# Scaling x by token ahead of time and splitting u on another engine, in the first stage of a hybrid decoder block

## The chip, the cores and the metric

The kernel runs on one core of a Trainium2 chip. A core has five engines with queues of their own: PE (TensorE, the matrix unit), DVE (VectorE), ACT (ScalarE), POOL (GpSimd) and SP (SyncE, which here only issues DMAs). Each engine works through its queue strictly in order; an instruction that waits holds up all that stands behind it on its engine. The metric is the device time of one execution in microseconds, the median of several runs.

## What is computed

One layer of a decoder block for 512 tokens of width 2048, in fp32. What matters here is its beginning:

```python
mod = jax.nn.silu(c) @ w_ada[l] + b_ada[l]          # (1, 12288): six vectors of 2048
sh1, sc1, g1, sh2, sc2, g2 = jnp.split(mod, 6, axis=-1)
u = _rmsnorm(h, norm_attn[l]) * (1 + sc1) + sh1     # 512 x 2048
z = u @ w_in                                        # then cut into queries, keys, values, gates
... two attentions, y @ w_out, a gated residual, SwiGLU, a last RMSNorm
```

`x` is (1, 512, 2048), `w_ada` (2048, 12288), `w_in` (2048, 5664).

## The kernel before

**Layout.** Activations lie transposed: a tile holds 128 features (partitions) by 512 tokens, so x and u are 16 tiles each (`xT`, `u`). To keep fp32 precision on fast matmuls every operand is split into a high part (rounded to fp32r) and a low part (the rest), and each product is three matmuls: high x high, low x high, high x low. ACT makes the high part and DVE the low part: of a weight chunk `wr` as `wh` (L244) and `wl` (L249), of u as `uh` (L416) and `ul` (L420).

**First stage.** x is loaded and transposed, and the token scale `rstd1` (one factor for each token) is made, in the first 25 us. Then 64 steps stream the two sixths of `w_ada` that give shift and scale, in eight blocks of eight steps. A step loads one tile `ad` of 128 x 2 x 512 (512 KB, in two DMAs). A block gives shift and scale of two feature tiles, and so two tiles of u. Within a block:

- DVE multiplies the rows of the `ad` tiles by SiLU(c) and adds them up in `acc` (L531 for the first, L533 for the others), two instructions for a tile; in some steps (`on_pe`) PE takes the second of the two as a matmul into a PSUM row (L540), which ACT copies out at the end (`row`, L544).
- Then PE sums over partitions (L552): eight small matmuls over `row`, eight over `acc`. The text calls this "the sums of block j".
- DVE adds the bias (`mod`, L560) and makes `a_vec` (L400), and for each of the two feature tiles `mt` = x * a_vec * rstd1 (L414). ACT makes `uh` from `mt` (L416), DVE then `ul` (L420).
- PE multiplies the new u with chunks of `w_in` in units of three matmuls (L278, L279, L280), 144 units in the stage. They go into eight PSUM banks: S0 (tags `pss`, `pso`, first for one half of the query columns, moved out by `keep_half` after block 3, then for the compressed keys and values) and S1 (`psmm`).

**What sets the order.** In this stage the queues stand as the code emits them. `LAGS` says how many steps after a block's last load its sums, its `mod`, its `ul` and its S1 units come; `KEEP` how many units may be left before a step emits two rather than one (three from block 4 on). `w_pairs` loads the chunks of `w_in` for a block (`wr`, at most three of a kind at a time), in the middle of a block. Eight `ad` tiles may be held at a time, so SP runs at most eight tiles ahead of DVE. The tables of sine and cosine (`extra_work`, L431 to L452) are made on DVE in blocks 1 to 3.

After the stage x is written to DRAM (`xsp`, L590), for which SP first has to issue three chunks of `w_in`, the last of which waits for a low part of block 7; the next stage goes on with the same u, and the rest of the kernel (attentions, FFN) isn't touched: from there on the instructions of both kernels stand in the same order on all engines.

Of the kernel before, what the change touches and what calls it, by code (L numbers as in the profile page):

```python
# [9 lines left out]
F32 = mybir.dt.float32  # L10
F32R = mybir.dt.float32r
I32 = mybir.dt.int32
AF = mybir.ActivationFunctionType
OP = mybir.AluOpType
AX = mybir.AxisListType

P = 128
T = 512
NT = T // P
D = 2048  # L20
ND = D // P
# [4 lines left out]
EPS = 1e-6  # L26
ADW = 8
LAG = 2
LAGS = 2, 3, 4, 6
LAGS0 = 1, 2, 3, 0  # L30
KEEP = 12
R_C, R_D, R_F, R_V = 1.0, 1.0, 1.0, 0.6
SCALE = HD ** -0.5
NCMP = 31
# [45 lines left out]
def hymba_block(ctx: ExitStack, tc: tile.TileContext, x, c, positions, w_ada, b_ada, norm_attn,  # L80
                norm_ffn, w_in, b_fgate, cmp_pos, w_kc1, w_kc2, w_vc1, w_vc2, beta_fox, beta_nsa,
                w_out, w_gate, w_up, w_down, final_norm, cst, out):
    nc = tc.nc
# [10 lines left out]
    act = pool(aw, "act")  # L94
# [7 lines left out]
    def uid(s):  # L102
        n_uid[0] += 1
        return f"{s}_{n_uid[0]}"
# [9 lines left out]
    def split_ap(t):  # L114
        return t.bitcast(F32)
# [287 lines left out]
    def act_tile(name, i):  # L403
        h = act.tile([P, T], F32R, tag="ah", name=uid(name + "h"), bufs=ND)
        l = act.tile([P, T], F32R, tag="al", name=uid(name + "l"), bufs=ND)
        return h, l

    def modulate(which, i, src, rb, pl):
        return modulate_b(*modulate_a(which, i, src, rb, pl))

    def modulate_a(which, i, src, rb, pl):
        sh = mod[:, (0 if which == 0 else 3) * ND + i:(0 if which == 0 else 3) * ND + i + 1]
        t = pl.tile([P, T], F32, tag="mt", name=uid("mt"), bufs=2)
        nc.vector.scalar_tensor_tensor(t, src, a_vec[:, which, i:i + 1], rb, op0=OP.mult, op1=OP.mult)  # L414
        h, l = act_tile("u", i)
        nc.scalar.activation(h, t, AF.Identity, bias=sh)  # L416
        return h, l, t, sh

    def modulate_b(h, l, t, sh):
        nc.vector.scalar_tensor_tensor(l, t, sh, split_ap(h), op0=OP.add, op1=OP.subtract)  # L420
        return h, l

    cosT = sinT = None

# [32 lines left out]
    p_cmp = [cols(w_in, C_KC, 512)]  # L457
    p_s1 = [cols(w_in, C_KS, 256), cols(w_in, C_KW, 128)]
    part = None
    u = []  # L460
    NJ = ND // 2
    HJ = NJ // 2

    def w_pairs(j):
        s1 = fetch_w(p_s1, j, src=early, width=3 * P, bufs=2)
        if j < HJ:
            return [fetch_w(p_qn, j), s1]
        i = 2 * (j - HJ)
        return [fetch_w(p_cmp, i), s1, fetch_w(p_cmp, i + 1)]
# [24 lines left out]

    def on_pe(n):
        j, r = divmod(n, 8)
        return r < 7 if j == 0 else 2 <= r < (6 if j <= HJ else 4)

    tiles, accs, rows, sums, halves, fetched, todo = {}, {}, {}, {}, {}, {}, []
    extra_work = tables()  # L500
    AT, AT_END = {0: 0, 1: 1, 3: 2}, {0: 0, 1: 1, 5: 2}
    step = 0
    while step < SLOTS + 8 or todo:
        j, r = divmod(step, 8)
        if j < NJ:
            tiles[step] = early.tile([P, 2, T], F32, tag="adw", name=uid("ad"), bufs=ADW)
            for i, sec in ((0, 1), (1, 0)):
                c0 = sec * D + j * 256
                nc.sync.dma_start(tiles[step][:, :, i * 256:(i + 1) * 256],
                                  w_ada[:, c0:c0 + 256].rearrange("(q p) n -> p q n", p=P)[:, 2 * r:2 * r + 2, :])  # L510
        if r == (2 if j else 7) and j < NJ:
            fetched[j] = w_pairs(j)
        if j == 1 and r < 2:
            fetched[0][r].high()
        i = AT.get(r, 3) if j < NJ else AT_END.get(r, 3)
# [7 lines left out]
        if 0 <= n < SLOTS:  # L523
            jj, q0 = n // 8, 2 * (n % 8)
            if q0 == 0:
                accs[jj] = early.tile([P, T], F32, tag="acc", name=uid("acc"), bufs=2)
            acc = accs[jj]
            for q in range(1 if on_pe(n) else 2):
                sc1 = sl[:, q0 + q:q0 + q + 1]
                if q0 + q == 0:  # L530
                    nc.vector.tensor_scalar(acc, tiles[n][:, q, :], sc1, None, op0=OP.mult)  # L531
                else:
                    nc.vector.scalar_tensor_tensor(acc, tiles[n][:, q, :], sc1, acc, op0=OP.mult, op1=OP.add)  # L533
        n = step - 2
        if 0 <= n < SLOTS and on_pe(n):
            jj, q = n // 8, 2 * (n % 8) + 1
# [10 lines left out]
        if n is not None:  # L547
            jj = n // 8
            sums[jj] = bank("mm")
            for av, one in ((rows.pop(jj), one_col[0:1, :]), (accs.pop(jj), one_col)):  # L550
                for i in range(4):
                    nc.tensor.matmul(sums[jj][:, i:i + 1], av[:, i * P:(i + 1) * P], one,  # L552
                                     start=one is not one_col and i == 0, stop=one is one_col,
                                     skip_group_check=True)
        n = due(step, 1)
        if n is not None:
            jj = n // 8
            for k2, sec in ((0, 1), (1, 0)):
                m0 = sec * ND + 2 * jj
                nc.vector.tensor_tensor(mod[:, m0:m0 + 2], sums[jj][:, 2 * k2:2 * k2 + 2], b_mod[:, m0:m0 + 2],  # L560
                                        op=OP.add)
            scale_vec(0, jj * 2, 2)
            pend = [modulate_a(0, i, xT[:, i, :], rstd1, early) for i in (2 * jj, 2 * jj + 1)]
            if jj == 0:
                halves[0] = [fetched[0][0]()]
        n = due(step, 2)
        if n is not None:
            u.extend([modulate_b(*h) for h in pend])
            jj = n // 8
            if jj == 0:  # L570
                halves[0].append(fetched[0][1]())
            if jj < HJ:
                todo += units(halves[jj][0], jj, S0, ND // 2) + units(halves[jj][1], jj, S1, ND)
            if jj == HJ - 1:
                todo.append(keep_half)
# [851 lines left out]
```

## Time and profile before

| | us |
|---|---|
| median of 3 runs | 2454.54 |
| lowest and highest | 2450.6 to 2454.8 |
| the profiled execution | 2450.92 |
| its span | 2448.0 |
| first stage, last matmul | 191.10 |

The profile belongs to one execution, and all sums below are made in it: its own time is 2.9 us over its span and 3.6 us under the median. To read it: busy times are sums over instructions; a row of the timeline gives start, duration, engine, line, and in brackets how long the engine had been idle and what it had waited for. A matmul's duration includes its way through the array, so the time that one matmul costs in a row of many is read from start to start. PEclk is the granted clock of TensorE as a share of 2.4 GHz; it has two levels, 1.2 and 2.4 GHz.

### The profile page before, as it was taken

The page shows a single profiled execution, that of the slowest core. Times are in us where ns is not written, and L with a number is a line of the kernel's source. Part 1 is how long each engine was busy: PE and PEld are TensorE (multiplying, and loading weights), DVE is VectorE, ACT ScalarE, POOL GpSimd, SP SyncE. Part 2 cuts the span into 40 slices and gives each one's busy share as a digit, 9 for nine tenths or more (in the row PEclk, how much of TensorE's full clock was granted, in tenths as well). Part 3 has the DMA queues.
Part 4 walks back from the last instruction along what each step waited for, and adds up shares of the span by engine and source line. Part 5 has one row for each costly group of instructions (what it writes and reads, how often), then busy time and mean ns, then how long its engine had stood idle before and what let it go on. Part 6 is the DMA issues. An engine that isn't in the chain of part 4 may idle for free.

```text
span 2448.0 us, 38482 instructions
## 1 busy us (share of the span) xinstructions
PE 2355.1 (96%) x14717; PEld 2100.4 (86%) x14717; DVE 1579.6 (65%) x2711; ACT 1016.0 (42%) x1531; POOL 341.5 (14%) x370
## 2 busy tenths in 40 slices
PE   6998999999999989889999999999999999999998
PEld 4677887888888767789999999999999888888887
DVE  6876786887755576596777777777776643333333
ACT  3224544344423332365555555555555422222133
POOL 0003002000001121251222121212221100000010
PEclk8998999999999999999999999999999999999999
DMA  9864743463554277559898989898988644333322
GB/s 332 283 198 147 205 139 95 130 190 117 180 174 129 85 249 253 186 122 237 211 231 215 228 213 232 220 225 212 221 200 193 192 151 141 123 120 121 102 95 101
DMA packets 322713, 440.31 MB, mean 180 GB/s; under 512 B 26224, under 2 KB 217552, under 8 KB 322528
## 3 DMA queue, kind: packets, MB, share of 16 engines
q1 hardware_dynamic: 289104, 348.21, 44.0%
q0 software_dynamic: 31120, 85.45, 18.7%
q10 hardware_dynamic: 2304, 4.20, 0.5%
q8 instruction: 115, 1.88, 0.3%
q14 instruction: 70, 0.57, 0.1%
HBM read 340.18 MB, written 28.38 MB: 151 GB/s over the span
## 4 chain that ended last, share of the span: by engine, by line
PE 54%; DVE 1%; DMA 0%; issue 0%; ACT 0%; SPq 0%; DVEq 0%; ACTq 0%
PE py L1161 12%; PE py L1164 11%; PE py L1163 11%; PE psmm L278 3%; PE psmm L279 3%; PE psmm L280 3%; PE pss L278 2%; PE pss L279 2%; PE pss L280 2%; PE pso L279 1%; PE pso L278 1%; PE pso L280 1%; DMA wr<-in_w_down_dram 0%; PE pso L1058 0%; DVE ul L1141 0%
## 5 line engine op out<-in xcount | busy, mean ns | idle before, releaser
L249 DVE TENSOR_TENSOR wl<-wr,wh 128x1024 fp32r<-128x1024 f32 (+2 forms) x211 | 239.0, 1133 | 381.5 <-ACT wh L244 378.4
L244 ACT CAST wh<-wr 128x1024 fp32r<-128x1024 f32 (+2 forms) x211 | 199.5, 948 | 502.7 <-PE psmm L279 199.7
L1164 PE MATMUL py<-uh,ls 128*128 128x256 f32 x1408 | 397.6, 282 | 3.6 <-DVE ls L1107 3.6
L1163 PE MATMUL py<-ul,hs 128*128 128x256 f32 x1408 | 397.6, 282 | 2.2 <-DVE ul L1141 2.2
L1161 PE MATMUL py<-uh,hs 128*128 128x256 f32 x1408 | 398.4, 283 | 1.0 <-DVE ev L1178 0.5
L1107 DVE TENSOR_TENSOR ls<-sum,hs 128x1024 fp32r<-128x1024 f32 x176 | 215.2, 1223 | 196.5 <-ACT hs L1101 196.5
L1101 ACT CAST hs<-sum 128x1024 fp32r<-128x1024 f32 x176 | 184.5, 1049 | 377.3 <-PE py L1163 257.5
L1163 PE MATMUL py<-ul,hx 128*128 128x256 f32 x1056 | 298.8, 283 | 4.0 <-DVE ul L1141 4.0
L1161 PE MATMUL py<-uh,hx 128*128 128x256 f32 x1056 | 299.3, 283 | 1.7 <-ACT uh L1140 1.4
L1164 PE MATMUL py<-uh,lx 128*128 128x256 f32 x1056 | 298.3, 282 | 0.0
L1164 PEld LDWEIGHTS py<-uh,ls 128*128 128x128 f32 x1408 | 267.0, 190 | 4.7 <-DVE ls L1107 4.6
L1163 PEld LDWEIGHTS py<-ul,hs 128*128 128x128 f32 x1408 | 267.0, 190 | 3.3 <-DVE ul L1141 3.3
L1161 PEld LDWEIGHTS py<-uh,hs 128*128 128x128 f32 x1408 | 267.1, 190 | 2.7 <-DVE ev L1178 1.3
L1097 POOL DMA_DIRECT2D lx<-raw x176 | 156.2, 887 | 580.2 <-ACT lx L1096 419.4
L1163 PEld LDWEIGHTS py<-ul,hx 128*128 128x128 f32 x1056 | 200.8, 190 | 5.1 <-DVE ul L1141 5.1
L1161 PEld LDWEIGHTS py<-uh,hx 128*128 128x128 f32 x1056 | 200.6, 190 | 2.2 <-ACT uh L1140 1.7
L1164 PEld LDWEIGHTS py<-uh,lx 128*128 128x128 f32 x1056 | 200.7, 190 | 0.0
L386 DVE SCALAR_TENSOR_TENSOR acc<-ad,sl,acc 128x512 f32<-128x512 f32 x180 | 141.6, 787 | 43.2 <-DMA ad<-in_w_ada_dram 41.4
L1092 ACT CAST hx<-raw 128x768 fp32r<-128x768 f32 x176 | 144.3, 820 | 11.3 <-DMA raw<-in_w_gate_dram 11.3
L1096 ACT ACTIVATE lx<-raw 128x768 fp32r<-128x768 f32 x176 | 148.1, 841 | 1.8 <-DMA raw<-in_w_gate_dram 1.8
L278 PE MATMUL psmm<-fh,wh 128*128 128x512 f32 x352 | 137.0, 389 | 0.0
L280 PE MATMUL psmm<-fh,wl 128*128 128x512 f32 x352 | 136.9, 389 | 0.0
(441 smaller groups left out, 5284.3 us busy)
## 6 DMA issues: line engine op xcount, KB each, us to landing
lx<-raw POOLq DMA_DIRECT2D x176, 384.0 KB, 5.2
ad<-in_w_ada_dram SPq DMA_DIRECT2D x128, 512.0 KB, 4.1
raw<-in_w_up_dram SPq DMA_DIRECT2D x176, 256.0 KB, 4.2
raw<-in_w_gate_dram SPq DMA_DIRECT2D x176, 256.0 KB, 4.5
wr<-in_w_down_dram SPq DMA_DIRECT2D x88, 512.0 KB, 3.6
ad<-in_w_ada_dram SPq DMA_DIRECT2D x128, 256.0 KB, 6.0
wr<-in_w_in_dram SPq DMA_DIRECT2D x104, 256.0 KB, 3.5
wr<-in_w_in_dram SPq DMA_DIRECT2D x24, 512.0 KB, 4.4
```

The lines of the kernel that those rows point to most:

```text
L244: nc.scalar.copy(wh[:, :, sc], v)
L249: nc.vector.tensor_tensor(held[1][:, :, sc], v, split_ap(held[0])[:, :, sc], op=OP.subtract)
L278: nc.tensor.matmul(dst, wh[:, k, w], ah, start=first, stop=False)
L279: nc.tensor.matmul(dst, wh[:, k, w], al, start=False, stop=False)
L280: nc.tensor.matmul(dst, wl[:, k, w], ah, start=False, stop=last)
L1096: nc.scalar.activation(lx[s], raw[s][:, 1:4, :], AF.Copy, scale=-1.0)
L1097: nc.gpsimd.dma_start(split_ap(lx[s]), raw[s][:, 1:4, :], accum_op=OP.add)
L1101: nc.scalar.copy(hs[s], sums[s])
L1107: nc.vector.tensor_tensor(ls[s], sums[s], split_ap(hs[s]), op=OP.subtract)
L1161: nc.tensor.matmul(o, wh[:, wi, js], vh[:, vi, :], start=k == 0 and j == 0, stop=False, skip_group_check=True)
L1163: nc.tensor.matmul(o, wh[:, wi, js], vl[:, vi, :], start=False, stop=False, skip_group_check=True)
L1164: nc.tensor.matmul(o, wl[:, wi, js], vh[:, vi, :], start=False, stop=k == KG - 1, skip_group_check=True)
```

## The change

- `norm_x` on DVE multiplies each of the 16 tiles of x by `rstd1` ahead of time, into `xn`, in steps 4 to 18 (blocks 0 to 2). `xn` uses the buffers that `ul` will have.
- ACT makes `uh` and `mt` from `xn` with a_vec as scale and the shift as bias, two instructions a tile (L418), and DVE `ul` = mt - uh as a plain subtraction (L423). `ul` comes five steps after the block's last load, not four (`LAGS`), and S1 units seven, not six. `KEEP` falls from 12 to 9.
- High parts of weights (`wh`) are cast by ACT two steps before DVE makes their low parts, so ahead of the copy of `row` and no longer behind it. `w_pairs` comes one step later.
- PE takes rows of `w_ada` in five steps of block 0 (seven before), four of blocks 1 to 4 as before, and none of blocks 5 to 7 (two each before). There `row` is gone, DVE takes both halves, and the sums are eight matmuls instead of sixteen.

```diff
-LAGS = 2, 3, 4, 6
+LAGS = 2, 3, 5, 7
-KEEP = 12
+KEEP = 9
...
-    def modulate_a(which, i, src, rb, pl):
-        sh = mod[:, (0 if which == 0 else 3) * ND + i:(0 if which == 0 else 3) * ND + i + 1]
-        t = pl.tile([P, T], F32, tag="mt", name=uid("mt"), bufs=2)
-        nc.vector.scalar_tensor_tensor(t, src, a_vec[:, which, i:i + 1], rb, op0=OP.mult, op1=OP.mult)
-        h, l = act_tile("u", i)
-        nc.scalar.activation(h, t, AF.Identity, bias=sh)
-        return h, l, t, sh
-
-    def modulate_b(h, l, t, sh):
-        nc.vector.scalar_tensor_tensor(l, t, sh, split_ap(h), op0=OP.add, op1=OP.subtract)
-        return h, l
+    u = []
+    xn = [act.tile([P, T], F32, tag="al", name=f"xn{i}", bufs=ND) for i in range(ND)]
+
+    def norm_x(i):
+        nc.vector.tensor_tensor(xn[i], xT[:, i, :], rstd1, op=OP.mult)
+
+    def modulate(i):
+        h = act.tile([P, T], F32R, tag="ah", name=uid("uh"), bufs=ND)
+        t = early.tile([P, T], F32, tag="mt", name=uid("mt"), bufs=2)
+        for dst in (h, t):
+            nc.scalar.activation(dst, xn[i], AF.Identity, scale=a_vec[:, 0, i:i + 1], bias=mod[:, i:i + 1])
+        return h, t
+
+    def modulate_low(h, t):
+        l = act.tile([P, T], F32R, tag="al", name=uid("ul"), bufs=ND)
+        nc.vector.tensor_tensor(l, t, split_ap(h), op=OP.subtract)
+        u.append((h, l))
...
-        return r < 7 if j == 0 else 2 <= r < (6 if j <= HJ else 4)
+        return r < 5 if j == 0 else j <= HJ and 2 <= r < 6
...
+    norms = {4: (0, 1), 5: (2,), 6: (3,), 8: (4, 5)}
+    norms.update({9 + i: (6 + i,) for i in range(10)})
...
-        if r == (2 if j else 7) and j < NJ:
+        if r == (3 if j else 7) and j < NJ:
             fetched[j] = w_pairs(j)
+        i = {7: 0, 0: 1, 1: 2}.get(r, 3)
+        if i < 3 and 1 <= j - (r < 7) < NJ and i < len(fetched[j - (r < 7)]):
+            fetched[j - (r < 7)][i].high()
...
+        if step in norms:
+            for i in norms[step]:
+                norm_x(i)
...
-            for av, one in ((rows.pop(jj), one_col[0:1, :]), (accs.pop(jj), one_col)):
+            srcs = ([(rows.pop(jj), one_col[0:1, :])] if jj in rows else []) + [(accs.pop(jj), one_col)]
+            for av, one in srcs:
...
-            pend = [modulate_a(0, i, xT[:, i, :], rstd1, early) for i in (2 * jj, 2 * jj + 1)]
+            pend = [modulate(i) for i in (2 * jj, 2 * jj + 1)]
...
-            u.extend([modulate_b(*h) for h in pend])
+            for p in pend:
+                modulate_low(*p)
```

Where the instructions stand now. First DVE, from the last `ad` tiles of block 0 to the first `ul`; `acc_292` and `acc_308` are block 0's sum, `wl_334` and `wl_357` the low part of the first chunk. Before:

```order
L533 SCALAR_TENSOR_TENSOR acc_292<-ad_320,sl,acc_292 128x512 x2
L531 TENSOR_SCALAR acc_356<-ad_330,sl 128x512
L533 SCALAR_TENSOR_TENSOR acc_356<-ad_330,sl,acc_356 128x512
L560 TENSOR_TENSOR mod<-psmm_341,vec 128x2 x2
L400 SCALAR_TENSOR_TENSOR a_vec<-mod,vec 128x2
L414 SCALAR_TENSOR_TENSOR mt_362<-xT,a_vec,rstd_269 128x512
L414 SCALAR_TENSOR_TENSOR mt_367<-xT,a_vec,rstd_269 128x512
L249 TENSOR_TENSOR wl_334<-wr_326,wh_333 128x1024
L533 SCALAR_TENSOR_TENSOR acc_356<-ad_350,sl,acc_356 128x512 x2
L420 SCALAR_TENSOR_TENSOR ul_365<-mt_362,mod,uh_364 128x512
```

and in the changed kernel:

```order
L540 SCALAR_TENSOR_TENSOR acc_308<-ad_343,sl,acc_308 128x512 x2
L412 TENSOR_TENSOR xn_282<-xT,rstd_269 128x512
L412 TENSOR_TENSOR xn_283<-xT,rstd_269 128x512
L538 TENSOR_SCALAR acc_378<-ad_353,sl 128x512
L540 SCALAR_TENSOR_TENSOR acc_378<-ad_353,sl,acc_378 128x512
L412 TENSOR_TENSOR xn_284<-xT,rstd_269 128x512
L571 TENSOR_TENSOR mod<-psmm_363,vec 128x2 x2
L400 SCALAR_TENSOR_TENSOR a_vec<-mod,vec 128x2
L249 TENSOR_TENSOR wl_357<-wr_349,wh_356 128x1024
L540 SCALAR_TENSOR_TENSOR acc_378<-ad_372,sl,acc_378 128x512 x2
L412 TENSOR_TENSOR xn_285<-xT,rstd_269 128x512
L423 TENSOR_TENSOR ul_400<-mt_386,uh_385 128x512
```

Three products of x by the token scale stand ahead of `mod`, one between it and the first `ul`, and the two `mt` behind `mod` are gone from DVE.

On ACT, block 1: the copy of `row`, the casts of the two chunks, and u. Before:

```order
L430 CAST posi<-posi 128x512
L544 COPY row_434<-psmm_403 1x512
L244 CAST wh_444<-wr_379 128x1024
L244 CAST wh_457<-wr_376 128x768
L416 ACTIVATE uh_492<-mt_490,mod 128x512
```

and in the changed kernel:

```order
L433 CAST posi<-posi 128x512
L244 CAST wh_465<-wr_417 128x1024
L554 COPY row_472<-psmm_432 1x512
L244 CAST wh_482<-wr_414 128x768
L418 ACTIVATE uh_523<-xn_280,mod,a_vec 128x512
L418 ACTIVATE mt_524<-xn_280,mod,a_vec 128x512
```

The first cast has moved ahead of the copy that waits for PE, and each tile of u has two instructions.

On PE, around the sums of block 7 (`row_1266`, `acc_1171`; now `acc_1196`). Before:

```order
L280 MATMUL psmm_282<-uh_1214,wl_1168 128x512
L552 MATMUL psmm_1324<-cs,row_1266 128x1 x4
L552 MATMUL psmm_1324<-cs,acc_1171 128x1 x4
L278 MATMUL psmm_283<-uh_1214,wh_1167 128x512
L279 MATMUL psmm_283<-ul_1215,wh_1167 128x512
```

and in the changed kernel:

```order
L280 MATMUL psmm_298<-uh_1225,wl_1175 128x512
L563 MATMUL psmm_1342<-cs,acc_1196 128x1 x4
L278 MATMUL psmm_299<-uh_1225,wh_1174 128x512
L279 MATMUL psmm_299<-ul_1267,wh_1174 128x512
L280 MATMUL psmm_299<-uh_1225,wl_1175 128x512
```

The sums over `row` are gone, and with them the matmuls over `ad` that fed them. Between the sums of successive blocks, from the start of u to the end of the stage, PE has 8, 11, 13, 17, 23, 24, 24 and 24 units before the change and 10, 11, 13, 15, 23, 24, 24 and 24 behind it.

## Rows read from the trace of the kernel before

**Rows 1.** Windows by block: busy us (count) of PE, PEld, DVE, ACT, POOL; clock, DMA, GB/s.

```profile
36.54:60.02 23.48, 17.14 (x55) 11.87 (x56) 18.23 (x29) 4.15 (x6) 0.00 (x0) 0.72 1.08 345
60.02:77.01 16.99, 14.79 (x59) 10.69 (x58) 16.81 (x31) 3.64 (x5) 0.00 (x0) 0.90 0.98 312
77.01:94.58 17.57, 16.23 (x64) 11.91 (x63) 16.40 (x29) 6.07 (x8) 0.00 (x0) 0.89 0.97 315
...
133.92:154.28 20.36, 20.36 (x93) 16.06 (x93) 16.32 (x24) 4.69 (x6) 0.00 (x0) 1.00 0.95 303
...
174.66:191.10 16.44, 16.44 (x72) 13.43 (x72) 5.64 (x9) 3.40 (x5) 0.00 (x0) 1.00 0.67 236
```

**Rows 2.** Waits of PE from 25 to 191 us: total, times, longest.

```profile
PE psmm L552 <- DVE acc L533: 5.5, 3, 2.2
PE psmm L552 <- ACT row L544: 3.1, 1, 3.1
PE pss L279 <- DVE ul L420: 2.4, 1, 2.4
...
PE pss L278 <- DVE part L482: 0.9, 1, 0.9
PE pss L278 <- ACT part L484: 0.8, 1, 0.8
```

**Rows 3.** Timeline of ACT, then DVE, then PE, around the sums of block 1.

```profile
51.70 0.58 ACT L544 COPY row<-psmm 1x512 f32<-1x512 f32 x1 [12.03 <-PE psmm L540]
52.19 1.77 ACT L244 CAST wh<-wr 128x1024 fp32r<-128x1024 f32 x2
...
53.26 1.23 DVE L249 TENSOR_TENSOR wl<-wr,wh 128x1024 fp32r<-128x1024 f32 x1 [4.86 <-ACT wh L244]
...
52.98 1.05 PE L552 MATMUL psmm<-cs,row 1*128 1x1 f32 x8
55.99 1.05 PE L552 MATMUL psmm<-cs,acc 128*128 128x1 f32 x8 [1.96 <-DVE acc L533]
...
57.48 0.63 PE L279 MATMUL psmm<-ul,wh 128*128 128x512 f32 x1
57.90 0.63 PE L280 MATMUL psmm<-uh,wl 128*128 128x512 f32 x1
...
61.33 1.02 PE L540 MATMUL psmm<-ad,sl 128*128 128x512 f32 x2
...
62.42 0.40 PE L279 MATMUL psmm<-ul,wh 128*128 128x512 f32 x1
```

**Rows 4.** Timeline of PE: sums of block 4 and the stage's last matmul.

```profile
109.99 1.05 PE L552 MATMUL psmm<-cs,row 1*128 1x1 f32 x8
110.96 1.05 PE L552 MATMUL psmm<-cs,acc 128*128 128x1 f32 x8
...
190.88 0.39 PE L280 MATMUL pso<-uh,wl 128*128 128x512 f32 x1
```

**Rows 5.** Timeline of DVE in block 0, then PE's first matmul with a low part.

```profile
30.41 1.54 DVE L533 SCALAR_TENSOR_TENSOR acc<-ad,sl,acc 128x512 f32<-128x512 f32 x2 [0.74 <-DMA ad<-in_w_ada_dram]
34.45 0.49 DVE L531 TENSOR_SCALAR acc<-ad,sl 128x512 f32<-128x512 f32 x1 [2.50 <-DMA ad<-in_w_ada_dram]
...
36.54 0.22 DVE L560 TENSOR_TENSOR mod<-psmm,vec 128x2 f32<-128x2 f32 x2 [0.81 <-PE psmm L552]
...
41.71 0.79 PE L279 MATMUL pss<-ul,wh 128*128 128x512 f32 x1 [2.36 <-DVE ul L420]
```

**Rows 6.** Groups of instructions, 25 to 191 us: busy us, mean ns, idle before.

```profile
L533 DVE SCALAR_TENSOR_TENSOR acc<-ad,sl,acc 128x512 f32<-128x512 f32 x89 | 66.7, 750 | 4.9 <-DMA ad<-in_w_ada_dram 2.9
L414 DVE SCALAR_TENSOR_TENSOR mt<-xT,a_vec,rstd 128x512 f32<-128x512 f32 x16 | 11.3, 748 | 0.4
L416 ACT ACTIVATE uh<-mt,mod 128x512 fp32r<-128x512 f32 x16 | 11.1, 724 | 53.3 <-DVE mt L414 53.3
```

**Rows 7.** Groups of instructions in the first 300 us: a subtraction of this shape.

```profile
L622 DVE TENSOR_TENSOR cA<-cr,cA 128x512 fp32r<-128x512 f32 x8 | 5.2, 686 | 0.1
```

More of the change, by code (lines that the diff above doesn't have):

```diff
@@ L406, in act_tile @@
         return h, l
-    def modulate(which, i, src, rb, pl):
-        return modulate_b(*modulate_a(which, i, src, rb, pl))
-    def modulate_a(which, i, src, rb, pl):
-        sh = mod[:, (0 if which == 0 else 3) * ND + i:(0 if which == 0 else 3) * ND + i + 1]
-        t = pl.tile([P, T], F32, tag="mt", name=uid("mt"), bufs=2)
-        nc.vector.scalar_tensor_tensor(t, src, a_vec[:, which, i:i + 1], rb, op0=OP.mult, op1=OP.mult)
-        h, l = act_tile("u", i)
-        nc.scalar.activation(h, t, AF.Identity, bias=sh)
-        return h, l, t, sh
-    def modulate_b(h, l, t, sh):
-        nc.vector.scalar_tensor_tensor(l, t, sh, split_ap(h), op0=OP.add, op1=OP.subtract)
-        return h, l
+    u = []
[12 more added lines that the diff above has]
+        u.append((h, l))
     cosT = sinT = None
@@ L459, in hymba_block @@
     part = None
-    u = []
     NJ = ND // 2
@@ L549, in hymba_block @@
             sums[jj] = bank("mm")
-            for av, one in ((rows.pop(jj), one_col[0:1, :]), (accs.pop(jj), one_col)):
+            srcs = ([(rows.pop(jj), one_col[0:1, :])] if jj in rows else []) + [(accs.pop(jj), one_col)]
+            for av, one in srcs:
                 for i in range(4):
                     nc.tensor.matmul(sums[jj][:, i:i + 1], av[:, i * P:(i + 1) * P], one,
-                                     start=one is not one_col and i == 0, stop=one is one_col,
+                                     start=i == 0 and one is srcs[0][1], stop=one is one_col,
                                      skip_group_check=True)
```

## The prediction

> **What bounds the kernel now.** I read the page first: PE is busy for most of the span, so what a change in the first stage is worth is time that PE gets back there. Then the windows cut at each block's `mod` [rows 1]. From the first `mod` at 36.54 us to about 110 us PE is busy for 73 to 92% of a block and DVE is nearly full in two blocks (16.81 of 16.99 us, 16.40 of 17.57), while the core loads 312 to 345 GB/s. From block 4's sums on it is the other way round: in the window from 133.92 us, one of three alike, PE is busy for all of the 20.36 us at the full clock, and DVE has time left. So there are two halves, paced by DVE and the chain of waits around it, and by PE.
>
> The list of PE's waits [rows 2] says what it lost in the first half: 5.5 us for `acc` in three sums, 3.1 us for `row`, 2.4 us for a first `ul`. The timeline of block 1 shows the chain [rows 3]: ACT stands 12.03 us at the copy of `row`, which waits for PE's last rows of `w_ada`; the casts queued behind it start at 52.19 us, DVE sits idle for 4.86 us until the first is done, the last `acc` stands behind that, and PE waits 1.96 us for it. Then matmuls start 0.42 us apart (57.48, 57.90) and later 0.24: the clock had fallen to 1.2 GHz. By the granted clock in rows 1 (0.72, 0.90, 0.89) some 20 us of these three blocks ran at the lower level.
>
> **Prices.** 72 matmuls took 16.44 us in the last window [rows 1]: 0.228 us each, 0.69 a unit. A `w_ada` row on PE: from 61.33 to 62.42 us stand two records of L540, one matmul of the program, and one of a unit [rows 3], so 1.09 - 0.23 = 0.86 us. Eight small sums: 109.99 to 110.96 us, 0.97 us [rows 4]. On DVE an `acc` step, `mt` and `ul` take 0.75 us and a subtraction of the same size 0.69 [rows 6, 7]; since their ends overlap, one costs 0.66 to 0.73 us and 0.61 from start to start.
>
> **From the sums of block 4 on.** Before, this takes 109.99 to 191.10 us [rows 4, 1], 81.1 us, with 95 units. The change takes off six rows of `w_ada`, 6 x 0.86 = 5.2 us, and three times eight sums over `row`, 2.9 us. Of the waits for `part` (0.9 and 0.8 us [rows 2]) about 1.4 us go: six units (4.1 us) now stand between the last unit that fills S0 and the first that needs it empty, and the two copies on ACT, behind a cast (1.0 us) and four activations (2.8 us), come 0.3 us too late. Left: 81.1 - 5.2 - 2.9 - 1.4 = 71.6 us. This needs DVE to keep up: its 16.32 us of block 6 [rows 1] lose two `mt` (1.4) and gain two `acc` steps (1.5), 16.4 to 16.8 us, against 24 units and 0.97 us on PE, 17.5 us. DMA must bring 5.6 MB a block (eight tiles, two chunks, one of 384 KB), 320 GB/s; rows 1 show 303 to 345 where nobody waited for it, and at 303 the block takes 18.6 us, 1.1 too long, which for three blocks comes out of the some 10 us by which tiles land ahead of their use. The added waits: a cast waits for its buffer until 14 units after the sums, then `wl` and the last `acc` follow (1.0 + 1.2 + 1.5 us), 3.5 us before PE needs them. Behind that cast on ACT stands only work of the next block.
>
> **From the first u to the sums of block 4.** Step by step, before in brackets.
> - Block 0. The idle 0.74 us of DVE before each tile [rows 5] takes the first products by `rstd1`; tile 7, here from 30.41 us, ends at 32.7 (31.95). Three products (1.8 us) and tile 8, which lands at 34.45 us, stand before `mod`: 36.3 us (36.54). `mt` is gone there, but a low part of a chunk, the next tile and one product stand before `ul`: it ends at 40.65 us, and PE's second matmul, which waits for it, goes then (41.71 [rows 5]).
> - Block 1. PE has ten units, not eight: the 11.3 us from 41.71 to 52.98 us [rows 5, 3] for eight units and four rows, partly at the low clock, and 1.4: 40.65 + 12.7 = 53.3 us. DVE's nine further products, 9 x 0.61 = 5.5 us, fill the hole of 4.86 us [rows 3], which is gone since the cast no longer stands behind `row`. Its last `acc` ends at 52.6 us, so PE doesn't wait for it. `mod` follows at 58.6 (60.02).
> - Block 2. PE has four units and a row after the sums (55.2 us), then needs a new u. `ul` follows `mod` by 3.6 us (three instructions of tables, two of `acc`, itself): 62.2 us. **PE stands 3.1 us** from 58.9, and I add 2.0 us for a clock at the lower level, as after the wait in rows 3. DVE needs 16.99 us less two `mt` and the shorter `ul`, 15.5: `mod` at 74.1 (77.01).
> - Blocks 3 and 4. DVE: 17.57 - 0.96 idle - 1.46 = 15.15, `mod` at 89.3 (94.58). PE has seven and eight units and three rows each before it needs a new u (7.4 and 8.1 us, against `ul` 4.3 and 4.6 us after the sums), so it doesn't stand. From 62.2 us: 35 units (24.2), 11 rows (9.5), two sums (3.9), clock 2.0, in all 39.6: **block 4's sums at 101.8 us (109.99)**. Without the lower clock 99.8; with a wait and a lower clock as in rows 3 (1.96 + 1.9) in both blocks 109.5.
>
> **Sum.** Stage end at 101.8 + 71.6 = 173.4 us against 191.1: 17.7 us. The next stage's first waits hang on `xsp`, which follows block 7's last `wl`; that comes 5.2 us after the sums' end rather than 4.9, since ACT now makes four activations (0.7 us each) before the last `ul`. That takes 0.4: 17.3 us. The profiled execution would take 2450.9 - 17.3 = 2433.6 us; the median lies 3.6 above it, so **2437 us**. ACT's sixteen further activations, 16 x 0.72 = 11.6 us, lie beside other work: ACT is busy for 4 to 6 us a block [rows 1].
>
> One price has no row: an activation with both scale and bias from memory. Bounds from rows are 0.72 us [rows 6], with the bias alone from memory, and 0.86, if the second operand adds what the first has over the plain copy of 0.58 us [rows 3]; less is excluded, since the work is the same. I take 0.72. The upper end moves `xsp` by four times 0.14, 0.6 us, and nothing else, since at the one stall DVE's own instructions end later than ACT's. The Trainium skill ("ScalarE: Activation LUTs", section "What ACT_TABLE_LOAD costs") says that each operand read per partition adds about 93 ns; by it four activations would take 0.4 us longer, an estimate from that page, and the sum would be 16.9 us instead of 17.3; no run here shows it yet.
>
> **Rivals.**
> - *DVE's chain takes over.* If products and tables make DVE 2 to 3 us later in blocks 2 and 3, the new u comes late there too, and PE stands and slows again. For it: the margins (about 3 us) are worked out, not measured, and the one sure stall shows how close it is. Against: every DVE piece there has a row. It takes away the 8.2 us of the first half: 2454.5 - 9.1 = 2445 us.
> - *DMA is the bound.* Loading was near its best in rows 1. At 300 GB/s, a little under the lowest of rows 1, the 37.3 MB behind tile 8 (55 tiles, 8.5 MB of `w_in`) need 124 us from 34.45 [rows 5], so block 7's sums come at 160.3 us, behind its last `acc`, and not at 155: 5 us of the gain go, 2443 us. Against: 345 GB/s in block 1, where buffers were free.
> - *The gain doesn't arrive*: the next stage's start is held by its own loads and `xsp`. SP issues these only behind chunks that wait for `wl` of block 7, so they should come as much earlier; if half were lost, 2446, if all, 2454.
> - *Slower.* PE stands at the sums of every block and falls to the lower clock each time. That is decided at DVE's block: above PE's 17.5 us, by 0.05 us more for each of its fifteen `acc` steps, `acc` comes last in blocks 5 to 7 too. A stop costs 1.96 us and ten matmuls at 0.42 instead of 0.23, 3.9 us [rows 3]; at the six sums from block 2 on 23.4 us, against 17.3 gained: 2460 us. The Trainium skill ("TensorE: Matmul & The Clock Gate", section "HAM oscillation — how this bites in real kernels") describes this, an engine that stands again and again and starts at the low clock each time; the trace agrees in blocks 1 to 3 and shows 1.00 in blocks 5 to 7, where PE never stood long.
>
> **How the numbers follow.** Chances: the sum 0.66 (2430 to 2442 by the clock in block 2, the price of an activation and the 4 us between the lowest and the highest run), DVE's chain 0.12, DMA 0.08, a lost gain 0.09 (half of it all lost), slower 0.05. The range reaches from 2430 to 2447, over the first three. A measurement of this kernel tells about 0.2% (4.9 us) from no change: faster 0.89, same 0.06, slower 0.05.
>
> **What would show it.** In the changed profile: DVE's idle time before `wl` for ACT (4.86 us in block 1) gone; no wait of PE for `acc` in sums 1 to 3; one wait for `ul` of about 3 us near 60 us, and the low clock behind it; block 4's sums near 102 us; from there PE busy without a gap at 17.5 us a block; last S0 matmul near 173 us. Wrong if PE waits for `acc` in blocks 5 to 7, if `ad` tiles land late, or if less than 17 us are left of the gain once the next stage runs.

## The result, and the profile after

| | us |
|---|---|
| before, median beside the changed kernel | 2454.67 |
| changed kernel, median of 4 runs | 2436.80 |
| lowest and highest | 2436.33 to 2438.08 |
| ratio to before, 95% interval | 0.9932, 0.9914 to 0.9949 |
| a second series of 5 runs beside other kernels: median, ratio | 2436.10, 0.9920 (0.9909 to 0.9932) |
| the profiled execution, its span | 2438.08, 2436.3 |
| first stage, last matmul | 175.1 |

The forecast of 2437 us stands within 1 us of both medians. Between the two profiled executions the difference is only 12.8 us, because the one of before lies 4 us under its median and the one of after 1 us above its own; so from here on the stage is measured by marks inside it.

The windows cut at each block's `mod` (columns as in [rows 1]), blocks 1 to 4, then 7 and the last units:

```profile
37.09:59.02 21.93, 16.91 (x63) 11.80 (x63) 21.75 (x37) 5.79 (x8) 0.00 (x0) 0.83 1.08 347
59.02:74.43 15.41, 13.89 (x54) 9.77 (x55) 15.27 (x29) 5.18 (x7) 0.00 (x0) 0.92 1.02 325
74.43:89.29 14.86, 14.86 (x63) 10.82 (x62) 14.68 (x26) 7.61 (x10) 0.00 (x0) 0.96 1.08 349
89.29:105.61 16.32, 16.32 (x66) 11.74 (x65) 12.25 (x20) 5.18 (x7) 0.00 (x0) 0.90 1.09 353
...
141.25:158.65 17.40, 17.40 (x81) 14.42 (x81) 13.46 (x21) 5.78 (x7) 0.00 (x0) 1.00 0.44 143
158.65:175.16 16.51, 16.51 (x73) 13.50 (x73) 4.10 (x7) 4.04 (x6) 0.00 (x0) 1.00 0.64 226
```

Against [rows 1] the blocks have shrunk from 23.48, 16.99 and 17.57 us to 21.93, 15.41 and 14.86; DVE is full in the first two (21.75 of 21.93, 15.27 of 15.41), PE from block 3 on. In the late blocks 17.40 us stand where 20.36 stood. The core now loads 325 to 353 GB/s in the early blocks, more than before.

PE's waits from 25 to 175 us (total, times, longest), then DVE's from 30 us:

```profile
PE pss L279 <- DVE ul L423: 3.4, 2, 2.2
PE pss L278 <- ACT uh L418: 2.4, 1, 2.4
PE psmm L550 <- issue: 1.9, 1, 1.9
PE psmm L563 <- DVE acc L540: 1.5, 1, 1.5
PE psmm L563 <- ACT row L554: 0.7, 1, 0.7
...
DVE wl L249 <- ACT wh L244: 6.0, 3, 2.7
DVE mod L571 <- PE psmm L563: 4.6, 2, 3.6
DVE ul L423 <- ACT mt L418: 3.0, 3, 1.6
```

The 5.5 us for `acc` in three sums [rows 2] have become 1.5 us in one, that of block 0, which lies ahead of the first u. Both waits for `part` are gone. The row to compare on DVE is its wait for a high part, 6.0 us in 3 waits now; before the change (30 to 191 us) it was 20.3 us in 11:

```profile
DVE wl L249 <- ACT wh L244: 20.3, 11, 5.4
```

The chain of [rows 3], block 1, now on ACT, DVE and PE:

```profile
51.88 0.57 ACT L554 COPY row<-psmm 1x512 f32<-1x512 f32 x1 [8.83 <-PE psmm L550]
...
50.46 1.22 DVE L249 TENSOR_TENSOR wl<-wr,wh 128x1024 fp32r<-128x1024 f32 x1
51.59 1.53 DVE L540 SCALAR_TENSOR_TENSOR acc<-ad,sl,acc 128x512 f32<-128x512 f32 x2
...
53.16 1.05 PE L563 MATMUL psmm<-cs,row 1*128 1x1 f32 x8
54.14 1.05 PE L563 MATMUL psmm<-cs,acc 128*128 128x1 f32 x8
...
59.34 1.10 PE L550 MATMUL psmm<-ad,sl 128*128 128x512 f32 x2 [1.94 <-issue]
62.56 0.50 PE L279 MATMUL pss<-ul,wh 128*128 128x512 f32 x1 [1.20 <-DVE ul L423]
```

ACT still stands behind PE for the copy of `row`, but the cast was done earlier: DVE makes `wl` at 50.46 us with no wait in front (4.86 us in [rows 3]), its `acc` follows, and PE's sums over `acc` stand directly behind those over `row`. The price is the last two rows: PE runs out of units and stands twice in block 2, 3.1 us in all. (For the first of the two the profile names no releaser, only "issue".)

### The profile page after: what moved, and what is told of

Read it like the earlier page. It is cut to its first block, busy times and chain, and to the rows that moved or that the text cites. A ratio compares the mean times of both kernels' runs of the same rounds, so it can differ in the third digit from the quotient of the medians.

```text
span 2436.3 us, 38417 instructions
## 1 busy us (share of the span) xinstructions
PE 2349.1 (96%) x14677; PEld 2100.5 (86%) x14677; DVE 1583.2 (65%) x2719; ACT 1026.5 (42%) x1544; POOL 341.2 (14%) x370
## 4 chain that ended last, share of the span: by engine, by line
PE 55%; DVE 1%; DMA 0%; issue 0%; ACT 0%; SPq 0%; DVEq 0%; ACTq 0%
PE py L1173 12%; PE py L1176 11%; PE py L1175 11%; PE psmm L278 3%; PE psmm L280 3%; PE psmm L279 3%; PE pss L278 2%; PE pss L279 2%; PE pss L280 2%; PE pso L278 1%; PE pso L279 1%; PE pso L280 1%; DMA wr<-in_w_down_dram 0%; PE pso L1070 0%; DVE ul L1153 0%
```

## Experiments

All are compared at marks that every kernel has: the first `mod` (36.0 to 38.4 us in the traces, since the landing of the early tiles differs), the sums of block 4, the next stage's first `r`, and the first matmul of L283 further on in that stage, the same instruction everywhere. "Low" counts the matmuls that run between 46 and 175 us, last 0.63 us and start 0.43 us apart, at the lower clock; each takes 0.2 us more than the 0.23 at the higher.

| kernel | median us | ratio to before (95%) | first `mod` to sums 4 | sums 4 to `r` | first `mod` to L283 | low |
|---|---|---|---|---|---|---|
| before | 2454.67 | | 73.5 | 85.9 | 181.4 | 23 |
| changed kernel | 2436.80 | 0.9932 (0.9914 to 0.9949) | 66.5 | 76.7 | 165.2 | 18 |
| after_again (the changed kernel, second trace) | 2436.10 | 0.9920 (0.9909 to 0.9932) | 64.9 | 75.5 | 162.4 | 6 |
| e1_rows_back | 2444.89 | 0.9955 (0.994 to 0.997) | 65.7 | 87.3 | 175.1 | 17 |
| e2_cast_late | 2457.43 | 1.0006 (0.9995 to 1.0017) | 73.4 | 85.5 | 180.9 | 28 |
| e3_u_on_dve | 2439.38 | 0.9934 (0.9917 to 0.9951) | 67.2 | 75.7 | 165.0 | 11 |
| e4_lags_back | 2439.94 | 0.9934 (0.9919 to 0.9948) | 68.5 | 75.4 | 166.0 | 18 |
| e5_rows_only | 2453.02 | 0.9988 (0.9976 to 0.9999) | 72.3 | 83.7 | 178.0 | 29 |
| e7_cast_only | 2444.87 | 0.9960 (0.9944 to 0.9975) | 68.5 | 83.5 | 174.1 | 14 |
| e10_third_cast | 2452.49 | 0.9988 (0.9976 to 1.0) | 73.2 | 82.8 | 178.2 | 29 |
| e8_sums_apart | 2433.51 | 0.9912 (0.9894 to 0.993) | | | 161.8 | 0 |
| e6_xsp_early | 2435.51 | 0.9910 (0.9898 to 0.9922) | 65.7 | 67.5 | 160.9 | 9 |
| e9_both | 2432.71 | 0.9903 (0.9891 to 0.9915) | | | 158.5 | 7 |
| e11_row_later | 2443.14 | 0.9945 (0.9933 to 0.9958) | 68.1 | 76.7 | 166.8 | 22 |

Ratios are to runs of before on the same chip in the same series, whose medians were 2454.67 to 2457.11. Where the sums are apart no single mark stands for them.

**The change without one of its parts.** Rows of `w_ada` back on PE as before the change, two more in block 0 and two in each of blocks 5 to 7:

```diff
-        return r < 5 if j == 0 else j <= HJ and 2 <= r < 6
+        return r < 7 if j == 0 else 2 <= r < (6 if j <= HJ else 4)
```

> The changed kernel with the rows of w_ada back on PE as before (seven steps of block 0, four of blocks 1 to 4, two of blocks 5 to 7); all else stays. Theory A (two halves: DVE and its chain of waits up to block 4's sums, PE from there): block 4's sums stay near 103.6 us; behind them PE has six rows more (6 x 0.86 = 5.2 us) and three times eight sums (2.9), so the stage's last S0 matmul comes at 175.1 + 8.1 = 183.2 us and the whole at 2436.8 + 8 = 2445 us. Theory B (DVE is the bound in blocks 5 to 7 too, since it took on those rows): DVE is relieved of 4.5 us, the two cancel in good part, and the last S0 matmul comes before 180 us. Theory C (the gain is nearly all from these rows, the other parts do little): 15 of the 16 us go, last S0 matmul near 190 us.

The stage's second half goes back to 87.3 us, the first keeps its gain. So the late blocks' part of the gain, some 10 us, belongs to the rows, given that all else is there. That is theory A; the stage ends at 185.0 us rather than its 183.2, and the clock fell once more, behind the sums of block 5 (seven low-clock matmuls, 1.4 us).

The early casts taken out:

```diff
-        i = {7: 0, 0: 1, 1: 2}.get(r, 3)
-        if i < 3 and 1 <= j - (r < 7) < NJ and i < len(fetched[j - (r < 7)]):
-            fetched[j - (r < 7)][i].high()
```

> The changed kernel without the early casts: the high part of a chunk is again cast where its low part is made, on ACT behind the copy of row. Theory A: in blocks 1 to 3 the chain row copy, cast, low part, last acc, sums is back; the low part waits for ACT again (4.9 us of DVE idle in block 1 before, less here since DVE has more to do), PE waits for acc in two or three sums, about 1.5 to 2 us each, and falls to the lower clock behind it (another 2 us each): block 4's sums at 108 to 113 us instead of 103.6, whole 2442 to 2446 us. Rival: DVE is so full of its own work in blocks 1 to 3 that the late cast costs nothing: block 4's sums within 1 us of 103.6, whole 2437.

A miss: nothing of the gain is left, in either half (73.4 and 85.5 us). Its timeline in block 5, first ACT, then DVE, then PE at the next sums:

```profile
137.18 0.80 ACT L418 ACTIVATE mt<-xn,mod,a_vec 128x512 f32<-128x512 f32 x1
137.88 1.03 ACT L244 CAST wh<-wr 128x1024 fp32r<-128x1024 f32 x1
...
134.84 0.16 DVE L400 SCALAR_TENSOR_TENSOR a_vec<-mod,vec 128x2 f32<-128x2 f32 x1
138.95 1.22 DVE L249 TENSOR_TENSOR wl<-wr,wh 128x1024 fp32r<-128x1024 f32 x1 [3.94 <-ACT wh L244]
...
151.74 1.32 PE L560 MATMUL psmm<-cs,acc 128*128 128x1 f32 x8 [2.84 <-DVE acc L537]
```

Without the early cast the third chunk's cast stands on ACT behind the four activations of u; DVE's `wl` stands directly behind `mod` and waits 3.94 us for it; with two more `acc` steps than before DVE's block then lasts 20.48 us (134.66 to 155.14), more than PE's 17.5, and PE waits for `acc` again. The work that the rows moved to DVE fits only because the casts no longer stop DVE.

u on DVE again as before the change, `mt` by one product of three factors behind `mod` and no `xn`:

```diff
-        for dst in (h, t):
-            nc.scalar.activation(dst, xn[i], AF.Identity, scale=a_vec[:, 0, i:i + 1], bias=mod[:, i:i + 1])
+        nc.vector.scalar_tensor_tensor(t, xT[:, i, :], a_vec[:, 0, i:i + 1], rstd1, op0=OP.mult, op1=OP.mult)
+        nc.scalar.activation(h, t, AF.Identity, bias=mod[:, i:i + 1])
```

> The changed kernel with u made as before: no products by the token scale ahead of time, mt on DVE from x, a_vec and rstd1 (one instruction a tile), one activation for uh, ul on DVE with the shift. All else stays. Theory A: moving the products ahead takes work from blocks 1 to 7 but fills blocks 0 to 2 with 16 x 0.61 = 9.8 us for 16 x 0.66 = 10.6 us taken off, so in the first half it is nearly an exchange: without it mod of block 1 comes some 4 us earlier (55 instead of 59), then every block takes 1.4 us more on DVE, and block 4's sums come within 1.5 us of 103.6. In blocks 5 to 7 DVE needs 18.2 us a block against 17.5 on PE and the sums wait about 0.7 us each: last S0 matmul 175 to 179, whole 2436 to 2441. Rival: the move of u to ACT is what makes the first half faster; without it block 4's sums fall back to 108 to 110 us and the whole to 2443 or more.

165.0 us to the mark lie between the changed kernel's two executions (162.4 and 165.2), with 11 low-clock matmuls between their 6 and 18. Less 0.2 us for each of these it is 162.8 against 161.2 to 161.6: what gave the change its name, scaling ahead and u on ACT, is worth some 1 to 2 us by these single traces. The medians lie 2.6 to 3.3 us apart, and the intervals of the ratios overlap.

The numbers of steps as before:

```diff
-LAGS = 2, 3, 5, 7
-KEEP = 9
+LAGS = 2, 3, 4, 6
+KEEP = 12
```

> The changed kernel with LAGS and KEEP as before (2, 3, 4, 6 and 12): ul and S1 units one step earlier, more units kept back. Theory A: PE's work is the same and it stands only before block 2's first u; with six units between the sums of block 1 and that u instead of four, the 3.1 us of waits there shrink to about 1.5, but two units less are done ahead of them; block 4's sums within 1.5 us of 103.6, whole within 2 us of 2436.8. Rival: the numbers matter, since with ul a step earlier DVE waits for ACT's fourth activation (0.8 us each) in every block, 1 to 1.6 us a block, which delays acc in blocks 1 to 3: block 4's sums at 106 to 108 us.

With as many low-clock matmuls as the changed kernel's first trace (18) it takes 0.8 us more to the mark. The effect is small, but its mechanism is the rival's: DVE waits for ACT's `mt` eight times (three in the changed kernel, 3.0 us), PE waits 2.76 us for `acc` at the sums of block 2, and block 4's sums come at 106.0 us. The median, 2439.94 us, lies outside theory A's 2 us. DVE from 30 us:

```profile
DVE ul L423 <- ACT mt L418: 6.0, 8, 1.6
```

One part of the change, the load of the chunks one step later (`w_pairs`), was not taken out by itself.

**One part alone, on the kernel before.** Rows only (the edit of `on_pe` and the sums without `row`), and casts only (the three lines above):

> The kernel before, with only the rows of w_ada taken off PE as in the change (none in blocks 5 to 7, five in block 0); casts, u and the numbers of steps as before. Theory A (the early cast is what lets the rows pay: without it DVE, with two more acc steps a block, waits behind its mod for the third chunk's cast, its block grows past PE's 17.5 us and PE waits for acc again): from the sums of block 4 to the next stage's first r 80 to 84 us (before 85.9, changed kernel 76.7), the first half as before (73.4 us from the first mod), total 2449 to 2453 us beside 2454.6. Theory B (the rows pay by themselves, and the late cast cost so much only because four activations of u stood ahead of it instead of two): 76 to 78 us, total 2445 to 2447.

> The kernel before, with only the early casts of the high parts; rows, u and the numbers of steps as before. Theory A (the early cast carries the first half): from the first mod to the sums of block 4 66 to 68 us (before 73.45), from there to the next stage's first r 85 to 86 as before, total 2447 to 2449 us. Theory B (the products made ahead are needed as well, since mt stands between mod and u on DVE): 70 to 72 us, total 2451 to 2453.

Rows alone: theory A holds; of the late 10 us only 2.2 come, and PE's list shows the reason: 8.4 us for `acc` in five sums. Casts alone give 7.3 us to the mark, 4.9 in the first half and 2.4 in the second, where the two waits for `part` are gone too. In the first half that is theory A within half a microsecond; the second half's 2.4 neither theory had, and 2444.87 us lies below both (its eight runs spread from 2442.79 to 2454.47). PE's waits with the rows alone, then with the casts alone (25 to 200 us):

```profile
PE psmm L553 <- DVE acc L533: 8.4, 5, 2.2
...
PE pss L278 <- DVE part L482: 2.5, 1, 2.5
```

```profile
PE psmm L555 <- DVE acc L536: 3.5, 2, 2.7
```

To the mark the rows alone give 3.4 us, the casts alone 7.3, both 16.4, since e3 is that with the numbers of steps (worth 0.8) and the later load of the chunks. The sum of the parts is 10.7; 5.7 us exist only together. Part of this is the clock: less 0.2 us for each low-clock matmul the three are 4.6, 5.5 and 14.0 us, and 3.9 are left. In the totals, where the ratios give some 3, 10 and 16 us, the rest of some 3 us is within the intervals. The other side of the same comparison is larger: by the ratios the casts are worth some 10 us on the kernel before, and 18 to 21 on the rest of the change (e2), where four activations of u rather than two stand ahead of the third chunk's cast.

**Which cast.** Only the third chunk's cast early, in blocks 4 to 7:

```diff
-        i = {7: 0, 0: 1, 1: 2}.get(r, 3)
+        i = {1: 2}.get(r, 3)
```

> The changed kernel with only the third chunk's cast early (blocks 4 to 7), the other casts late as before the change. Theory A (the run with all casts late lost the second half by this one cast, which stood behind four activations, and the first half by the first cast behind the copy of row): first half about 73 us as before, from the sums of block 4 to the first r 76 to 78 (85.5 with all casts late, 76.7 in the changed kernel), total 2446 to 2449 us. Theory B (in the second half too the casts behind the copy of row and behind the sums are what costs): 82 us or more, total 2452 or more.

Theory B holds (82.8 us, total 2452.49). Blocks 6 and 7 do recover, as the last two of these windows show, but blocks 4 and 5 don't; windows by block, then DVE and PE:

```profile
99.20:119.73 20.53, 19.42 (x84) 14.25 (x82) 12.25 (x21) 6.24 (x8) 0.00 (x0) 0.99 0.94 299
119.73:141.46 21.73, 18.05 (x76) 14.91 (x77) 17.30 (x27) 6.71 (x9) 0.00 (x0) 0.92 0.80 247
141.46:157.91 16.45, 15.50 (x73) 12.61 (x72) 16.02 (x26) 5.78 (x7) 0.00 (x0) 1.00 0.86 271
157.91:172.96 15.05, 15.05 (x72) 12.52 (x71) 13.54 (x21) 5.78 (x7) 0.00 (x0) 1.00 0.49 165
```

```profile
109.15 1.23 DVE L249 TENSOR_TENSOR wl<-wr,wh 128x1024 fp32r<-128x1024 f32 x1 [2.88 <-ACT wh L244]
...
116.09 0.96 DVE L249 TENSOR_TENSOR wl<-wr,wh 128x768 fp32r<-128x768 f32 x1 [4.27 <-ACT wh L244]
...
123.41 0.75 PE L278 MATMUL pss<-uh,wh 128*128 128x512 f32 x1 [4.79 <-DVE part L484]
```

There DVE waits for the other two casts, one behind the copy of `row` (107.59 us on ACT), one from 114.27 us; `mod` is late, the copies of `part` stand behind it on DVE, and PE waits 4.79 us for them. Each late cast costs where it stands, not one of them alone.

**The clock behind the sums.** The eight sums over `row` one step ahead of the eight over `acc`, and the changed kernel once more:

```diff
+        n = due(step + 1, 0)
+        if n is not None and n > 7 and n // 8 in rows:
+            jj = n // 8
+            sums[jj] = bank("mm")
+            sum_up(rows.pop(jj), one_col[0:1, :], True, False)
```

> The changed kernel with the eight sums over row one step ahead of the eight over acc in blocks 1 to 4, two to three units between them. Theory A (the clock falls behind the sums of blocks 3 and 4 because sixteen matmuls of one column stand in a row for 1.9 us): no matmuls 0.43 us apart near 90 and near 107 us, sums of block 4 about 2 us earlier, the stage's end 3 us earlier, total about 2434 us. Theory B (the clock falls for another reason, as the waits before): the slower stretches stay, total 2436 to 2438. Should PE wait for the copy of row, up to 1 us a block is lost again, which shows as a wait for row.

> The changed kernel once more, unchanged, beside the other three on the same chip: total 2436 to 2440 us; from the first mod to the first r 143 us within 0.5 us, and from there to the end of the span 2253 to 2260 us, which shows how much of a difference between totals the rest of the kernel makes by itself. The clock that fell behind the sums of blocks 3 and 4 falls again if it hangs on where the sums stand (both times), and elsewhere or not if it is chance.

In the changed kernel's first trace the clock falls behind the sums of blocks 2, 3 and 4, with no wait of PE:

```profile
87.02 1.05 PE L563 MATMUL psmm<-cs,acc 128*128 128x1 f32 x8
...
89.29 0.63 PE L280 MATMUL pso<-uh,wl 128*128 128x512 f32 x1
89.72 0.63 PE L278 MATMUL psmm<-uh,wh 128*128 128x512 f32 x1
...
92.81 0.39 PE L279 MATMUL psmm<-ul,wh 128*128 128x512 f32 x1
```

In its second trace the same instructions at the same place keep the clock:

```profile
87.35 1.05 PE L563 MATMUL psmm<-cs,acc 128*128 128x1 f32 x8
...
89.28 0.39 PE L279 MATMUL pso<-ul,wh 128*128 128x512 f32 x1
89.51 0.39 PE L280 MATMUL pso<-uh,wl 128*128 128x512 f32 x1
```

So it differs between executions, and one trace decides nothing; the second trace's first `r` comes 140.4 us after the first `mod`, not the 143 expected. Counted over blocks 1 to 4 in five traces: with sixteen sums in a row the clock fell behind 6 of 12 (3, 1 and 2 in the changed kernel, its second trace and e6), with the sums apart behind 1 of 8 (none in e8, one in e9). In e8 the granted clock is 1.00 in each window of blocks 2 to 4. Less 0.2 us for each low-clock matmul the changed kernel takes 161.2 to 161.6 us, e8 161.8 with none: what the spacing gives, it gives through the clock alone. The median is lower with it both times, by 2.6 to 3.3 us (2433.51 beside 2436.10 and 2436.80, 2432.71 beside 2435.51), but the intervals of the ratios overlap. The other kernels widen the count. In the twelve traces whose sums stand in a row, with no wait over 0.2 us at them, the clock fell behind 13 of 32 in blocks 1 to 4 and 1 of 9 in blocks 5 to 7; where PE had waited 0.27 to 2.8 us at the sixteen sums, behind all 16. Theory A fits this, but 1 of 8 against 13 of 32 doesn't settle it.

**The next stage's start.** The writes of x issued earlier, alone and with the sums apart:

```diff
+        if step == SLOTS:
+            for i in range(ND):
+                nc.sync.dma_start(xsp[i], xT[:, i, :])
...
-    for i in range(ND):
-        nc.sync.dma_start(xsp[i], xT[:, i, :])
```

> The changed kernel with the sixteen writes of x to DRAM issued when SP has issued its last ad tile, ahead of the next stage's three chunks of w_in, instead of behind them. In the changed kernel DVE waits 1.79 us for these writes (to 179.22 us), the next stage's first r follows at 180.23, PE waits 2.30 us for it and then runs matmuls 0.43 us apart for 3.4 us. Theory A (the writes hold r): the first r 1.5 to 2 us earlier, PE's wait for r under 1 us, total 2433 to 2435 us beside the changed kernel's 2436.8. Theory B (the writes now stand ahead of the chunks, which come late): PE waits for a high part of w_in near 176 us, total 2436 to 2440. Theory C (r is held by the last matmul into its bank and by ACT): 0.5 us or less.

> The sums over row one step ahead of those over acc, as in the run with the sums apart, and the early writes of x together. If each takes away a loss of its own: the first r near 139.8 - 1.8 = 138 us after the first mod (changed kernel 143.1, sums apart 139.8), total about 2431 to 2432 us. If the earlier end of the stage meets the next stage's loads instead, a new wait for a high part of w_in stands there and the total stays at 2433 to 2434.

The changed kernel's DVE and PE at the stage's end, then those of the kernel with early writes:

```profile
179.22 0.17 DVE L697 MEMSET ht<- 128x128 f32 x1 [1.79 <-DMA xsp<-xT]
...
180.23 0.69 DVE L623 SCALAR_TENSOR_TENSOR r<-psmm,cosT 128x512 f32<-128x512 f32 x1 [0.64 <-ACT sw L622]
...
180.97 0.63 PE L278 MATMUL psmm<-uh,wh 128*128 128x512 f32 x1 [2.30 <-DVE r L623]
```

```profile
169.43 0.17 DVE L698 MEMSET ht<- 128x128 f32 x1 [6.04 <-PE psmm L280]
...
170.60 0.69 DVE L624 SCALAR_TENSOR_TENSOR r<-psmm,cosT 128x512 f32<-128x512 f32 x1 [0.79 <-ACT sw L623]
...
182.26 0.50 PE L280 MATMUL psmm<-uh,wl 128*128 128x512 f32 x1 [1.56 <-DVE wl L249]
```

Counted from the first `mod`, the first `r` comes 9.9 and 7.2 us earlier than in the changed kernel's two traces (133.2 us beside 143.1 and 140.4), not 2: it now follows PE's last unit into its bank (169.43 us). PE's wait for it is gone; a wait of 1.56 us for a low part has come, which DVE now makes behind more of the next stage's work. At the mark 1.6 to 4.3 us are left (160.9 beside 162.4 and 165.2), in the median 0.6 to 1.3; the total, 2435.51 us, lies just above theory A's 2433 to 2435. Both edits together reach 158.5 us at the mark and 2432.71 us, the lowest median of all, 3.4 to 4.1 us below the changed kernel; the two intervals overlap here too. Neither forecast for them is met as it stands: the total lies between the two, and the new wait is for a low part, not for a high one.

**PE's stand in block 2.** Block 2's rows on PE one step later:

```diff
-        return r < 5 if j == 0 else j <= HJ and 2 <= r < 6
+        return r < 5 if j == 0 else j <= HJ and 2 + (j == 2) <= r < 6 + (j == 2)
```

> The changed kernel with block 2's four rows of w_ada on PE one step later, so that no row of block 2 needs the PSUM bank of block 1's sums before mod has read it. In the changed kernel PE stands 1.94 us in front of such a row and 1.20 us for ul. Theory A (the stand is DVE's: PE has only four units before it needs the new u, whatever the bank does): one wait for ul of 3 to 4 us that ends at the same time after the first mod (25.5 us), stage end within 1 us of the changed kernel's, total 2436 to 2438. Theory B (the bank is a wait of its own): the two stands together shrink by 1.5 to 2 us and the stage's end comes as much earlier, total 2434 to 2435.

The wait in front of the row is gone, and one wait for `ul` stands there, 2.57 us; PE, then DVE:

```profile
64.11 0.79 PE L279 MATMUL pss<-ul,wh 128*128 128x512 f32 x1 [2.57 <-DVE ul L423]
...
62.70 0.74 DVE L540 SCALAR_TENSOR_TENSOR acc<-ad,sl,acc 128x512 f32<-128x512 f32 x1
63.37 1.28 DVE L423 TENSOR_TENSOR ul<-mt,uh 128x512 fp32r<-128x512 f32 x2
```

It ends 26.3 us after the first `mod` (25.5 in the changed kernel), 0.8 later, since the step that PE no longer takes puts one more `acc` (0.74 us) ahead of `ul` on DVE. So the stand is DVE's, as theory A says. The total isn't its 2436 to 2438: the mark comes 1.6 and 4.4 us later than in the changed kernel's two traces, 0.8 of it by that `acc` and 0.8 and 3.2 by more low-clock matmuls (22 against 18 and 6). The median lies further off, 6.3 to 7.0 us above the changed kernel's; what the marks leave of that no trace here explains.

## Why the prediction was right, point by point

Times are counted from the first `mod`, predicted at 36.3 and measured at 37.09 us; over all traces that instruction wanders by 2.4 us with the landing of the early tiles, which no step could foresee.

- **The cast off the chain.** Right. DVE's wait for ACT in block 1 (4.86 us) is gone, PE waits for `acc` in none of sums 1 to 3. e2 shows that this is the step on which all rests: with late casts the whole gain is gone. The prediction counted the cast in the first half only and treated the late blocks as safe ("this needs DVE to keep up"), where the same early casts keep DVE's block under PE's; it never said what the block would be without them.
- **Blocks 1 to 3.** `mod` was predicted 22.3, 37.8 and 53.0 us after the first; it came after 21.93, 37.34 and 52.20.
- **The stand of 3.1 us in block 2.** Right in size (1.94 + 1.20), by DVE's `ul`, as e11 shows. By the prediction's own marks (62.2 less 58.9) it would be 3.3; the sum goes on from 62.2 and doesn't change. Not foreseen: most of it shows at the row of `w_ada`, whose PSUM bank is by the program the one that block 1's sums hold until `mod` has read them (`mod` starts at 59.02 us, PE goes on at 59.34).
- **The clock.** The mis-sized term. Predicted: one fall, behind that stand, 2.0 us. Measured: none behind the stand in either trace, but three falls behind sums without a stand in the first trace (18 low-clock matmuls, 3.6 us), one in the second (6, 1.2 us). Of the 18, 11 stand ahead of block 4's sums (2.2 us) and 7 behind them (1.4), where the prediction had none. Block 4's sums were to come 65.5 us after the first `mod`; they came after 66.5 and 64.9.
- **From the sums of block 4.** 71.6 us predicted; 71.5 measured in the first trace (103.55 to 175.1) and 70.4 in the second; 17.40 us a block against 17.5. Of the first trace's 71.5 the seven low-clock matmuls are 1.4, so the term was some 1 us too large and the clock hid it. Both waits for `part` went, 1.7 us, not 1.4. The three late windows before the change that the prediction calls alike are not quite: in that from 113.80 us PE was busy for 18.46 of 20.12, and the waits for `part` lie in it.
- **xsp.** The first `r` 5.1 us behind the stage's end, 4.76 before: 0.4 predicted, 0.38 measured. That the first `r` could be had 7 to 10 us earlier by moving these writes was in no step.
- **The activation with two operands from memory.** 0.72 us taken, 0.80 to 0.81 measured (groups of L418: 808 and 801 ns). The step was 0.08 us too low, inside its bounds. It costs less than four times that at the last `ul`, since the four start 0.70 to 0.72 us apart: block 7's run from 159.04 to 161.99 us, 2.95 us against 4 x 0.72 = 2.88. The Trainium skill's page "ScalarE: Activation LUTs" (section "What ACT_TABLE_LOAD costs") gives about 93 ns for such an operand; for the single instruction the trace (0.08 us) agrees with it better than with the prediction's choice, but the 0.4 us that the prediction worked out from it for four in a row did not come.
- **The rivals.** DMA: 325 to 353 GB/s and no wait of DVE for a tile behind 37 us. DVE's chain in blocks 2 and 3: DVE is full there, but PE is too from block 3. Slower by stops: PE doesn't stop at the sums any more. The run with late casts comes nearest to this rival, with seven waits for `acc`, 10.8 us in all, and 28 low-clock matmuls, and still it is not slower than before. It is also the run nearest to what the Trainium skill's page "TensorE: Matmul & The Clock Gate" (section "HAM oscillation — how this bites in real kernels") describes, stops that each bring the low clock back: there the clock fell behind four of the six such waits from block 1 on. The gain that doesn't arrive: 15.6 us are left at the first `r` in the first trace, under the 17 that the prediction asked for, and 18.1 in the second (181.4 - 162.4 = 19 at L283); the twelve low-clock matmuls more, 2.4 us, are nearly all of the difference.

The mechanism was right; that the total hit 2437 within 1 us is partly luck. The sum of the steps, 17.3 us, stands against 17.9 and 20.6 between the medians of the two series, the two traces of the changed kernel differ by 2.8 us at the mark, and in the first of them the clock and the term for the stage's second half missed in opposite directions.

## What to carry to other kernels

An engine that has slack on average can still stop another one by what stands ahead of a short instruction in its queue; move the instruction ahead of the wait before you move work between engines. Two edits that lift bounds taking turns (a chain, then an engine's load) can be worth more together (16.4 us to the mark) than apart (3.4 and 7.3; some 4 us of the difference remain without the clock), so an edit that gives little alone isn't thereby shown to be worthless. Compare a stage from a mark inside it to a mark behind it, and take a second trace before a fall of the clock is explained.

## What the runs showed of the hardware

- The clock can fall without any wait of PE: behind sixteen matmuls of one column in a row matmuls went from 0.23 to 0.43 us apart for some 1.3 to 3 us, at 14 of 41 places in twelve traces, and not at the same places in two executions of one kernel. Where PE had waited 0.27 to 2.8 us at those sums, it fell at all 16 places; behind eight alone without such a wait, in the late blocks, at none of 26.
- On ACT a plain copy of 128 x 512 out of PSUM took 0.57 to 0.58 us (`part`), an `ACTIVATE` of this shape 0.72 with one operand from memory [rows 6] and 0.80 to 0.81 with two; four of the last in a row started 0.70 to 0.72 us apart.
- From the mark L283 to the end of the span, where all kernels have the same instructions, the traces take 2230 to 2239 us. No difference between totals below that spread can be put down to an edit from one trace.
